# Weights of two small products in two-tile buffers, their splits moved between VectorE and GpSimd, a norm laid out later, and padded operands cleared once

## The chip, the core and the metric

The kernel runs on one core of a Trainium2 chip. A core has TensorE (PE in the profile; PEld is its weight load), VectorE (DVE), ScalarE (ACT), GpSimd (POOL) and SyncE (SP), which here issues the transfers from HBM. SBUF is the working memory of 128 partitions, PSUM holds the products of TensorE in eight banks. The metric is the device time of one execution in microseconds (us), as a median over runs.

## What is computed

One layer of a first model (a gated delta rule beside a linear recurrent unit, then a feed-forward with a squared ReLU) works on 256 tokens of width 1,024. Then 16 learned tokens are put in front, and two layers of a second model follow. The change touches that second model most:

```python
def hybrid_mixer(u, w_in, w_attn_out, conv_w, conv_b, conv_ln_g, conv_ln_b, w_conv_out, w_out):
    proj = u @ w_in
    q, k, v, a, b, g_sb, g_conv = jnp.split(proj, IN_SPLITS, axis=-1)
    y_sb = stick_breaking_attention(q, k, v) @ w_attn_out
    y_conv = conformer_conv(a, b, conv_w, conv_b, conv_ln_g, conv_ln_b) @ w_conv_out
    m = jax.nn.sigmoid(g_sb) * y_sb + jax.nn.sigmoid(g_conv) * y_conv
    return m @ w_out

def second_block(x, meta, ...):
    h = jnp.concatenate([meta_b, x], axis=1)
    for l in range(DEPTH_2):
        h = h + 0.5 * swiglu(rmsnorm_2(h, ffn1_norm[l]), ffn1_w_gate[l], ffn1_w_up[l], ffn1_w_down[l])
        h = h + hybrid_mixer(rmsnorm_2(h, mix_norm[l]), w_in[l], ...)
        h = h + 0.5 * swiglu(rmsnorm_2(h, ffn2_norm[l]), ffn2_w_gate[l], ffn2_w_up[l], ffn2_w_down[l])
    h = rmsnorm_2(h, final_norm)
    return h[:, N_META:]
```

The attention has 8 heads of 64 columns and weighs a key by a sigmoid and the running product of the sigmoids behind it; `conformer_conv` is a gated convolution over 31 tokens, a layer norm and a SiLU. All numbers are float32.

## The kernel before, in words

Everything is held transposed: a tile has 128 features on the partitions and the tokens (256, or 272 with the learned ones) along the free dimension. The residual stream `H` has 8 such tiles and stays in SBUF. A weight tile is 128 by 128.

**Products in three parts.** TensorE multiplies in a reduced float32 format. So each weight tile is split into a high part (`wh`, a copy by ScalarE, line 276) and a low part (`wl`, weight minus high, by VectorE on line 288 or by GpSimd on line 493), and each input too (`x` high and low). One product is three matmuls, high by high, high by low, low by high (lines 534 to 536).

**Jobs and units.** `plan()` lists all products in order as jobs: one job makes one output tile of 128 features. `layout()` cuts a job into units of up to 8 weight tiles (1,024 columns) and packs units into transfers of up to 2,048 columns (`chunks`). Units of `ys` (attention output, `w_attn_out`) and `yc` (convolution output, `w_conv_out`) have only 4 tiles, 512 columns. A job puts its matmuls in a PSUM bank; the first two jobs of `ff1`, of `o2` (output product, `w_out`) and of gate and up are made as a pair, six tiles of each and then two of each.

**Buffers and splits.** There are 5 `wh` and 4 `wl` buffers of 1,024 columns, one per unit in turn. A split is laid out when the unit that is 2 ahead is forced (`MINLEAD`), or up to 3 ahead (`LEAD`) when the plan sees VectorE free. `POOLED` says which units are split on GpSimd: every fourth of the mixer's input products, every second of the list of `ys` and `o2` units, all of `yc`.

**The order of the work** is made while the program is built. Each engine's queue is in order. `op()` keeps a clock per engine with a cost per instruction. The rest of the work, evacuations, norms, attention heads, is written as generators (`flows`); after each weight tile `tick()` lets those go on that are ready by these clocks. `force()` runs flows until a condition holds.

**The stages around the change.** After `o1` (the first layer's output product) `residual` adds into `H`, makes the next input `x` and sums its squares into `acc1`, on GpSimd (`add=pt`). `norm_rows` makes token sums of `acc1` on TensorE (line 319), an inverse root in twelve small VectorE operations, and rows of it by four or six small products. In the mixer the order is `a`/`b`, `q`/`k`, `v`, the gates `gc`, `gs`, then `ys`, `yc`, `o2`. `do_ys` multiplies by a gate out of PSUM; `do_yc` does the same, adds both (SBUF with SBUF) and splits the sum into `mo`, the input of `o2`: a ScalarE copy and a VectorE subtraction. `layer_norm` makes `CO`, the input of `yc`. Behind `o2`, `residual` makes the input of the next gate and up products.

**Padded operands.** Queries of two heads share a tile; `QZ[i]` holds one head of each pair with zeros in the other half. `VZ` holds the values with zero columns between the heads, `AM` the attention weights of the 16 learned tokens with zero rows. All lie in the mixer's arena (`MIX2` columns, opened anew in each layer) and are cleared by GpSimd at its start (lines 1482 to 1484).

Of the kernel before, what the change touches and what calls it, by code (L numbers as in the profile page):

```python
# [23 lines left out]
MIX2 = 16200  # L24
XW = 320
SKEW = ((64, 0), (0, 32))
HSKEW = {"ff1": (56, 32), (0, 0): (56, 16), (1, 0): (56, 32), (0, 1): (56, 48), (1, 1): (56, 16)}
LEAD = 3
# [6 lines left out]
POOLED = [(("a", "b", "q", "k", "v", "gc", "gs"), 4), (("ys", "o2"), 2), (("yc", ), 1), (("o1b",), 2), (("K", "Q"), 8)]  # L35
# [73 lines left out]

def layout():  # L110
# [3 lines left out]
    for j, (_, _, _, _, _, kts) in enumerate(plan()):  # L114
        mine = []
        for ks in kts:
            n = 128 * len(ks)
            limit = 1024 if len(chunks) <= 2 else CHUNK_COLS
            if not chunks or chunks[-1][1] + n > limit:
# [106 lines left out]
def tile_hybrid_blocks(  # L226
# [11 lines left out]
    jobs = plan()  # L238

# [148 lines left out]
    def tick():  # L388
# [8 lines left out]
        while st["split"] < min(st["unit"] + LEAD + 1, len(units)) and clk["V"] < clk["P"] + AHEAD:  # L397
            emit_split(st["split"])
# [64 lines left out]
    for kinds, every in POOLED:  # L463
        mine = [i for i, u in enumerate(units) if jobs[u[0]][0] in kinds]
        on_pool.update(mine[every - 1::every])

    def emit_high(u):
        while st["high"] <= min(u, len(units) - 1):
            i = st["high"]
            _, ks, c, o = units[i]  # L470
            emit_dma(c)
            n = 128 * len(ks)
# [10 lines left out]
    def emit_split(u):  # L483
        while st["split"] <= min(u, len(units) - 1):
            i = st["split"]
            emit_high(i + (i > 0))
            _, ks, c, o = units[i]
            n = 128 * len(ks)
# [12 lines left out]
            if i + 1 < len(units) and units[i + 1][2] != c:  # L501
                raw.pop(c)
                emit_dma(c + RAW - 1)
# [4 lines left out]
    def job(kind, x, n, o=0, bank_=None, last=True, start=None):  # L508
# [14 lines left out]
        for u in mine:  # L523
            st["unit"] = u
            emit_split(u + MINLEAD)
            h, lo = wh.pop(u), wl.pop(u)
            clk["P"] = max(clk["P"], w_at.pop(u) + LAT)
            for i, k in enumerate(units[u][1]):
# [3 lines left out]
                s = slice(128 * i, 128 * i + 128)  # L532
# [795 lines left out]
    start_flow(norm_rows(acc1[:, 0:T1], T1, 1.0 / 1024, 1e-6, R[:, 0:T1], [ev_sq2], ev_r2))  # L1328
# [86 lines left out]

    def swiglu(x, ev_r, o, n, next_g, old_phase, skew, final=False):
# [28 lines left out]
        for m in range(FF2):  # L1445
# [5 lines left out]
            start_flow(evac(ga, ua, m))  # L1451
        x.done()
# [12 lines left out]
    def mixer(x, ev_r, layer, next_g, old_phase):  # L1465
# [9 lines left out]
        QZ = [arena.get(4, n) for _ in range(2)]  # L1475
# [3 lines left out]
        VZ = arena.get(3, 4, 192)  # L1479
        AM = [arena.get(n) for _ in range(2)]  # L1480
        for i in range(2):
            nc.gpsimd.memset(QZ[i].f[64 * (1 - i):64 * (1 - i) + 64], 0.0)  # L1482
# [386 lines left out]
```

## Time and profile before

| | |
|---|---|
| median of 3 runs | 1536.48 us (1528.25 to 1539.7) |
| profiled execution, its own time | 1534.88 us |
| its span, first to last instruction | 1533.2 us |
| mean granted TensorE clock | 0.989 |
| PE busy | 1490.7 us, 97%, 12,120 matmuls |
| VectorE busy | 1075.5 us, 70% |
| ScalarE busy | 802.5 us, 52% |
| GpSimd busy | 196.4 us, 13% |
| HBM read | 245.63 MB |

Busy time of an engine includes the time in which an instruction has begun and is held by something else. A row of the timeline gives start, duration, engine, line, operation, output and inputs, shapes, and in square brackets how long the engine had been idle before it and what it waited for. A row of a window gives a stretch, its length, and for each engine its busy time and the instructions in it, then the granted clock. The matmuls overlap in the pipeline: one of 256 columns is shown with some 0.28 us though they follow each other every 0.11 to 0.12 us, so the pace is read from their count, not from their duration.

### The profile page before, as it was taken

How to read it: one execution, taken by the hardware profiler on the slowest of the kernel's cores; microseconds unless marked ns; L12 is line 12 of the kernel's file. 1: busy time of each engine (PE TensorE's matmuls, PEld its weight loads, DVE VectorE, ACT ScalarE, POOL GpSimd, SP SyncE). 2: the span in 40 equal slices, each digit the busy share in tenths (PEclk: the TensorE clock that was granted, in tenths of full speed). 3: DMA queues.
4: the chain of work that ended last, by engine and by line, in shares of the span. 5: the costliest groups of instructions: out<-in, count | busy, mean ns of one | idle time of the engine just before them, and what ended most of it. 6: DMA issues, size and time to landing. Idle time of an engine off the chain costs nothing. (4 is left out here: it accounts for less than half of the span.)

```text
span 1533.2 us, 29451 instructions
## 1 busy us (share of the span) xinstructions
PE 1490.7 (97%) x12120; PEld 1470.4 (96%) x12120; DVE 1075.5 (70%) x1882; ACT 802.5 (52%) x1365; POOL 196.4 (13%) x236
## 2 busy tenths in 40 slices
PE   7999999999999999999999999999999999899997
PEld 7888999999999999998999999999999989899997
DVE  5986876667666568998866555666558997776654
ACT  4568666544544445555644444444444655555542
POOL 3330300000000012234400000000003235400000
PEclk8999999999999999999999999999999999999998
DMA  5412455554545544433545454554554423455551
GB/s 220 144 56 84 154 204 189 174 190 141 215 166 174 178 171 144 156 114 111 177 182 188 162 177 160 192 184 171 176 186 149 155 110 138 152 207 193 187 181 71
DMA packets 36376, 248.58 MB, mean 162 GB/s; under 512 B 3984, under 2 KB 5264, under 8 KB 12304
## 3 DMA queue, kind: packets, MB, share of 16 engines
q1 hardware_dynamic: 35248, 245.50, 45.3%
q8 instruction: 95, 1.56, 0.4%
q10 hardware_dynamic: 992, 1.19, 0.2%
q14 instruction: 41, 0.34, 0.1%
HBM read 245.63 MB, written 1.05 MB: 161 GB/s over the span
## 5 line engine op out<-in xcount | busy, mean ns | idle before, releaser
L534 PE MATMUL bank<-x,wh 128*128 128x272 f32 (+1 forms) x2752 | 795.8, 289 | 10.7 <-ACT x L276 9.8
L535 PE MATMUL bank<-x,wh 128*128 128x272 f32 (+1 forms) x2752 | 785.3, 285 | 6.5 <-DVE x L288 5.9
L536 PE MATMUL bank<-x,wl 128*128 128x272 f32 (+1 forms) x2752 | 786.8, 286 | 4.2 <-DVE wl L288 3.3
L288 DVE TENSOR_TENSOR wl<-raw,wh 128x1024 fp32r<-128x1024 f32 (+4 forms) x453 | 531.0, 1173 | 191.0 <-PE bank L536 159.5
L276 ACT ACTIVATE wh<-raw 128x1024 fp32r<-128x1024 f32 (+4 forms) x510 | 494.4, 975 | 268.0 <-issue 135.0
L534 PEld LDWEIGHTS bank<-x,wh 128*128 128x128 f32 x2752 | 523.5, 190 | 14.0 <-ACT x L276 10.8
L535 PEld LDWEIGHTS bank<-x,wh 128*128 128x128 f32 x2752 | 524.2, 190 | 9.7 <-DVE x L288 8.0
L536 PEld LDWEIGHTS bank<-x,wl 128*128 128x128 f32 x2752 | 522.0, 190 | 5.5 <-DVE wl L288 4.4
L536 PE MATMUL bank<-hid,wl 128*128 128x272 f32 (+1 forms) x960 | 273.1, 285 | 0.0
L535 PE MATMUL bank<-hid,wh 128*128 128x272 f32 (+1 forms) x960 | 273.0, 284 | 0.0
L534 PE MATMUL bank<-hid,wh 128*128 128x272 f32 (+1 forms) x960 | 272.4, 284 | 0.0
L535 PEld LDWEIGHTS bank<-hid,wh 128*128 128x128 f32 x960 | 181.3, 189 | 0.0
L536 PEld LDWEIGHTS bank<-hid,wl 128*128 128x128 f32 x960 | 180.8, 188 | 0.0
L534 PEld LDWEIGHTS bank<-hid,wh 128*128 128x128 f32 x960 | 180.4, 188 | 0.0
L493 POOL TENSOR_TENSOR wl<-raw,wh 128x512 fp32r<-128x512 f32 (+3 forms) x57 | 106.4, 1878 | 191.9 <-PE bank L536 89.7
L288 DVE TENSOR_TENSOR tmp<-bank,R 128x272 f32<-128x272 f32 (+1 forms) x184 | 78.9, 430 | 66.6 <-PE bank L536 65.8
L276 ACT ACTIVATE tmp<-tmp 128x272 f32<-128x272 f32 (+1 forms) x140 | 59.3, 425 | 114.8 <-DVE tmp L288 78.6
L299 DVE SCALAR_TENSOR_TENSOR bank<-arena,C,bank 128x272 f32<-128x272 f32 (+1 forms) x232 | 102.5, 492 | 3.7 <-ACT bank L276 2.5
L1482 POOL MEMSET arena<- 64x1088 f32 (+1 forms) x4 | 3.9, 976 | 769.0 <-PE bank L536 769.0
L288 DVE TENSOR_TENSOR hid<-tmp,hid 128x272 fp32r<-128x272 f32 (+1 forms) x120 | 51.7, 433 | 38.0 <-ACT hid L276 38.0
L276 ACT ACTIVATE x<-H,C 128x272 fp32r<-128x272 f32 (+2 forms) x64 | 30.0, 487 | 84.7 <-DVE H L288 84.3
L276 ACT ACTIVATE hid<-tmp 128x272 fp32r<-128x272 f32 (+1 forms) x120 | 51.0, 426 | 42.3 <-DVE tmp L288 40.6
(200 smaller groups left out, 950.5 us busy)
## 6 DMA issues: line engine op xcount, KB each, us to landing
raw<-in_w_dram SPq DMA_DIRECT2D x187, 1024.0 KB, 4.8
raw<-in_w_dram SPq DMA_DIRECT2D x32, 960.0 KB, 4.7
raw<-in_w_dram SPq DMA_DIRECT2D x16, 896.0 KB, 4.6
raw<-in_w_dram SPq DMA_DIRECT2D x2, 512.0 KB, 5.9
H<-in_xt_dram SPq DMA_DIRECT2D x1, 544.0 KB, 6.6
LG<-in_lgw_dram SPq DMA_DIRECT2D x1, 512.0 KB, 6.1
out_dram<-H SPq DMA_DIRECT2D x2, 256.0 KB, 2.3
LM<-in_cm_dram SPq DMA_DIRECT2D x1, 320.0 KB, 5.1
```

Source lines behind the costliest of these rows:

```text
L276: nc.scalar.activation(out, in_, func, scale=scale, **kw)
L288: nc.vector.tensor_tensor(out=out, in0=a, in1=b, op=fn)
L299: nc.vector.scalar_tensor_tensor(out=out, in0=a, scalar=s, in1=b, op0=op0, op1=op1)
L493: nc.gpsimd.tensor_tensor(out=lo[:, 0:n], in0=raw[c][:, o:o + n], in1=wh[i][:, 0:n].bitcast(F32), op=SUB)
L534: nc.tensor.matmul(acc, h[:, s], xh, start=first and done == 0, stop=False)
L535: nc.tensor.matmul(acc, h[:, s], xl, start=False, stop=False)
L536: nc.tensor.matmul(acc, lo[:, s], xh, start=False, stop=last and done == total - 1)
L1482: nc.gpsimd.memset(QZ[i].f[64 * (1 - i):64 * (1 - i) + 64], 0.0)
```

## The change

1. `SHARED = ("ys", "yc")`: two jobs in turn of one of these kinds share one pair of buffers of 1,024 columns (a "load"). `layout()` keeps both in one transfer. Splits, look-ahead and `POOLED` now count loads; a product reads its half of the buffer at `o_w`.
2. `POOLED`: `ys` and `o2` are off GpSimd; of `yc`, every second load (of two tiles) stays there, which is two per layer.
3. `residual` behind `o2` sums squares on VectorE (`add=pt` is gone).
4. `norm_rows` behind `o1` is started after the fifth `ff1` job and no longer ahead of `ff1`.
5. `QZ` and `VZ` live in a pool `held` of their own, opened behind `ff2`, and are cleared once, by GpSimd, after the ninth gate/up pair of the first SwiGLU. `AM` is cleared in each mixer as before. `MIX2` falls from 16,200 to 11,800 columns. The pools opened later (`hid` of the SwiGLUs, the mixer's arena) lie higher in SBUF by the size of `held`: 2 x 4 x 272 + 3 x 4 x 192 = 4,480 columns of 4 bytes.

```diff
-MIX2 = 16200
+MIX2 = 11800
+SHARED = ("ys", "yc")
-POOLED = [(("a", "b", "q", "k", "v", "gc", "gs"), 4), (("ys", "o2"), 2), (("yc", ), 1), (("o1b",), 2), (("K", "Q"), 8)]
+POOLED = [(("a", "b", "q", "k", "v", "gc", "gs"), 4), (("yc",), 2), (("o1b",), 2), (("K", "Q"), 8)]
...
+            both = 2 * n if kind in SHARED and nth_of_kind(j) % 2 == 0 else n
+            if not chunks or chunks[-1][1] + both > limit:
...
+    loads, load_of = [], []
+    for u, (j, ks, c, o) in enumerate(units):
+        if jobs[j][0] in SHARED and nth_of_kind(j) % 2:
+            loads[-1][2] += 128 * len(ks)
+            load_of.append((len(loads) - 1, 128 * len(ks)))
+        else:
+            loads.append([c, o, 128 * len(ks), jobs[j][0]])
+            load_of.append((len(loads) - 1, 0))
...
-        while st["split"] < min(st["unit"] + LEAD + 1, len(units)) and clk["V"] < clk["P"] + AHEAD:
+        while st["split"] < min(load_of[st["unit"]][0] + LEAD + 1, len(loads)) and clk["V"] < clk["P"] + AHEAD:
...
-            emit_split(u + MINLEAD)
-            h, lo = wh.pop(u), wl.pop(u)
+            i, o_w = load_of[u]
+            emit_split(i + MINLEAD)
+            h, lo = wh[i], wl[i]
...
-                s = slice(128 * i, 128 * i + 128)
+                s = slice(o_w + 128 * i, o_w + 128 * i + 128)
...
-    start_flow(norm_rows(acc1[:, 0:T1], T1, 1.0 / 1024, 1e-6, R[:, 0:T1], [ev_sq2], ev_r2))
...
+        if m == 4:
+            start_flow(norm_rows(acc1[:, 0:T1], T1, 1.0 / 1024, 1e-6, R[:, 0:T1], [ev_sq2], ev_r2))
...
+    ff1_phase.close()
+    held_pool = ctx.enter_context(tc.tile_pool(name="held", bufs=1))
+    QZ = [held_pool.tile([128, 4, T2], F32, name=f"qz{i}") for i in range(2)]
+    VZ = held_pool.tile([128, 3, 4, 192], F32, name="vz")
+    zeroed = []
+    def zeros():
+        for i in range(2):
+            nc.gpsimd.memset(QZ[i][64 * (1 - i):64 * (1 - i) + 64], 0.0)
+        nc.gpsimd.memset(VZ, 0.0)
...
+            if m == 8 and not zeroed:
+                zeroed.append(True)
+                zeros()
...
-        QZ = [arena.get(4, n) for _ in range(2)]
-        VZ = arena.get(3, 4, 192)
-        for i in range(2):
-            nc.gpsimd.memset(QZ[i].f[64 * (1 - i):64 * (1 - i) + 64], 0.0)
-            nc.gpsimd.memset(AM[i].f, 0.0)
-        nc.gpsimd.memset(VZ.f, 0.0)
+        for a in AM:
+            nc.gpsimd.memset(a.f, 0.0)
...
-            start_flow(residual(b, m, nx, next_g(m), acc1[:, 0:n], ev_sq, o, add=pt))
+            start_flow(residual(b, m, nx, next_g(m), acc1[:, 0:n], ev_sq, o))
```

More of the change, by code (lines that the diff above doesn't have):

```diff
@@ L107, in plan, with nth_of_kind @@
     return jobs
+def nth_of_kind(j):
+    jobs = plan()
+    n = 0
+    while n < j and jobs[j - n - 1][0] == jobs[j][0]:
+        n += 1
+    return n
 def layout():
@@ L113, in layout @@
     off = 0
-    for j, (_, _, _, _, _, kts) in enumerate(plan()):
+    for j, (kind, _, _, _, _, kts) in enumerate(plan()):
         mine = []
@@ L118, in layout @@
             limit = 1024 if len(chunks) <= 2 else CHUNK_COLS
-            if not chunks or chunks[-1][1] + n > limit:
+            both = 2 * n if kind in SHARED and nth_of_kind(j) % 2 == 0 else n
+            if not chunks or chunks[-1][1] + both > limit:
                 if chunks:
@@ L463, in tile_hybrid_blocks @@
     for kinds, every in POOLED:
-        mine = [i for i, u in enumerate(units) if jobs[u[0]][0] in kinds]
+        mine = [i for i, load in enumerate(loads) if load[3] in kinds]
         on_pool.update(mine[every - 1::every])
     def emit_high(u):
-        while st["high"] <= min(u, len(units) - 1):
+        while st["high"] <= min(u, len(loads) - 1):
             i = st["high"]
-            _, ks, c, o = units[i]
+            c, o, n, _ = loads[i]
             emit_dma(c)
-            n = 128 * len(ks)
             h = whp.tile([128, 1024], F32R, tag="wh", name="wh")
@@ L483, in emit_split @@
     def emit_split(u):
-        while st["split"] <= min(u, len(units) - 1):
+        while st["split"] <= min(u, len(loads) - 1):
             i = st["split"]
             emit_high(i + (i > 0))
-            _, ks, c, o = units[i]
-            n = 128 * len(ks)
+            c, o, n, _ = loads[i]
             lo = wlp.tile([128, 1024], F32R, tag="wl", name="wl")
@@ L500, in emit_split @@
             st["split"] += 1
-            if i + 1 < len(units) and units[i + 1][2] != c:
+            if i + 1 < len(loads) and loads[i + 1][0] != c:
                 raw.pop(c)
@@ L1507, in keep_q @@
                 p = slice(64 * i, 64 * i + 64)
-                cp(QZ[i].f[p, t], b[p, 0:n])
+                cp(QZ[i][p, t, 0:n], b[p, 0:n])
             give(b)
@@ L1620, in head @@
                 S = t0 + tn
-                mm(b[:, col:col + S], QZ[par].f[:, hp, t0 - o:t0 - o + 128], KT.f[:, hp, 0:S])
+                mm(b[:, col:col + S], QZ[par][:, hp, t0 - o:t0 - o + 128], KT.f[:, hp, 0:S])
                 col += S
@@ L1672, in head @@
             py = pairs[hp][0]
-            V = VZ.f[:, :, hp, 64 * par:64 * par + 128]
+            V = VZ[:, :, hp, 64 * par:64 * par + 128]
             e = n - 256
```

4 lines of the change are left out of this document (2 added, 2 removed).

## The prediction, made before the change was run

> **What bounds the kernel now.** I read the page first, then the list of what TensorE waited for, then windows around each of those waits, then the order of time on VectorE, GpSimd (POOL) and TensorE inside them.
>
> ```profile
> PE 1490.7 (97%) x12120; PEld 1470.4 (96%) x12120; DVE 1075.5 (70%) x1882; ACT 802.5 (52%) x1365; POOL 196.4 (13%) x236
> ```
>
> TensorE is busy for 97% of the span, and the change takes no product away. It can only win places where TensorE waits or is slowed. These are the windows of the stages that the change touches (columns: length, then busy time and count of PE, PEld, DVE, ACT, POOL, then granted clock, DMA share, GB/s); the first and the last are undisturbed and give the pace.
>
> ```profile
> 390.00:470.00 80.00, 80.00 (x645) 80.00 (x645) 47.63 (x68) 37.95 (x54) 0.00 (x0) 1.00 0.50 183
> 710.70:714.40 3.70, 2.76 (x13) 1.83 (x13) 2.35 (x7) 3.60 (x8) 0.22 (x1) 1.00 0.20 80
> 714.40:733.10 18.70, 17.10 (x122) 16.68 (x122) 17.40 (x27) 9.68 (x19) 10.91 (x8) 0.91 0.46 155
> 1282.70:1305.80 23.10, 22.19 (x194) 21.94 (x194) 17.80 (x32) 15.09 (x28) 15.03 (x11) 1.00 0.46 151
> 1305.80:1323.50 17.70, 11.92 (x74) 11.12 (x74) 14.11 (x20) 8.89 (x16) 8.28 (x5) 0.81 0.48 168
> 1323.50:1337.60 14.10, 14.10 (x122) 14.10 (x121) 9.04 (x14) 7.12 (x15) 6.21 (x6) 1.00 0.36 141
> ```
>
> A product takes 80/645 = 0.124 us at 272 columns and 14.10/122 = 0.116 us at 256. So layer 0 loses 3.7 - 12 x 0.124 = 2.2 us at its first `yc` job and 18.7 - 120 x 0.124 = 3.8 us from there to the second `o2` job; layer 1 loses 23.1 - 192 x 0.116 = 0.9 us over `ys` and `yc`, and 17.7 - 72 x 0.116 = 9.4 us in the first five `o2` jobs (window counts include products cut by the edges). What these losses are made of shows in layer 1, VectorE first, then GpSimd, then TensorE:
>
> ```profile
> 1304.76 0.95 DVE L288 TENSOR_TENSOR wl<-raw,wh 128x768 fp32r<-128x768 f32 x1
> 1305.63 0.42 DVE L288 TENSOR_TENSOR x<-arena,x 128x256 fp32r<-128x256 f32 x1
> 1305.96 0.41 DVE L288 TENSOR_TENSOR arena<-arena,bank 128x256 f32<-128x256 f32 x1
> 1306.41 1.86 DVE L288 TENSOR_TENSOR arena<-arena 128x256 f32<-128x256 f32 x1
> 1308.20 0.41 DVE L288 TENSOR_TENSOR arena<-arena,bank 128x256 f32<-128x256 f32 x1
> 1308.64 0.42 DVE L288 TENSOR_TENSOR arena<-arena 128x256 f32<-128x256 f32 x1
> 1308.98 0.42 DVE L288 TENSOR_TENSOR x<-arena,x 128x256 fp32r<-128x256 f32 x1
> 1306.16 1.83 POOL L493 TENSOR_TENSOR wl<-raw,wh 128x768 fp32r<-128x768 f32 x1 [2.73 <-ACT wh L276]
> 1314.68 2.57 DVE L288 TENSOR_TENSOR x<-arena,x 128x256 fp32r<-128x256 f32 x1
> 1314.58 2.38 POOL L493 TENSOR_TENSOR wl<-raw,wh 128x1024 fp32r<-128x1024 f32 x1 [2.76 <-ACT wh L276]
> 1317.30 0.58 PE L535 MATMUL bank<-x,wh 128*128 128x256 f32 x1 [3.62 <-DVE x L288]
> ```
>
> The same 0.42 us addition takes 1.86 us where a GpSimd split lies over it and ends just after that split; the low half of `mo` takes 2.57 us under a 2.38 us split, and TensorE waits 3.62 us for it. An operation with a PSUM operand is not held:
>
> ```profile
> 718.61 0.42 DVE L288 TENSOR_TENSOR arena<-arena,bank 128x272 f32<-128x272 f32 x1
> 718.35 4.40 POOL L493 TENSOR_TENSOR wl<-raw,wh 128x512 fp32r<-128x512 f32 x3
> ```
>
> So the cost of a GpSimd split in these stages is VectorE's waiting, more than the split. Behind the long waits the clock falls:
>
> ```profile
> 725.20:728.60 3.40, 1.80 (x14) 1.38 (x12) 3.33 (x6) 1.15 (x4) 1.83 (x1) 1.00 0.54 224
> 728.60:732.00 3.40, 3.40 (x15) 3.40 (x16) 3.07 (x8) 2.20 (x6) 0.73 (x1) 0.51 0.37 80
> 1315.70:1319.10 3.40, 1.80 (x8) 1.80 (x9) 2.46 (x2) 1.06 (x1) 1.26 (x1) 0.51 0.27 63
> ```
>
> TensorE busy for 1.80 of 3.4 us was enough to halve the clock in the next 3.4 us, which costs 1.7 us. The Trainium skill ("TensorE: Matmul & The Clock Gate", Part 1) halves the clock after a whole idle window of about 3.4 us; by that rule no halving would be left after this change and the sum below would not move, but the trace halves it earlier, so a leftover wait of near 2 us is priced below with 1.7 us on top.
>
> **The change part by part.**
>
> *First norm moved behind the fifth `ff1` job.* Its token sums stand in TensorE's queue ahead of the third `ff1` job:
>
> ```profile
> 182.78 0.61 PE L319 MATMUL bank<-ones,acc 128*128 128x1 f32 x4 [2.06 <-POOL acc L311]
> ```
>
> Moved past three jobs of 24 products (about 8 us), the sums find `acc1` finished long before; `R2` is read only behind all 32 jobs. VectorE's twelve small operations and the four row products move along and cost the same. Gain 2.1 us, bounds 1.5 to 2.1 (the next weights might be late instead).
>
> *Zeroing once.* At the start of each mixer GpSimd clears two `QZ`, two `AM`, `VZ` and small borders, and only then makes the split of the second `b` tile that is queued behind. GpSimd, then VectorE, then TensorE, layer 0:
>
> ```profile
> 559.58 1.00 POOL L1482 MEMSET arena<- 64x1088 f32 x1 [376.25 <-PE bank L536]
> ...
> 562.13 2.02 POOL L1484 MEMSET arena<- 128x2304 f32 x1
> ...
> 564.47 2.39 POOL L493 TENSOR_TENSOR wl<-raw,wh 128x1024 fp32r<-128x1024 f32 x1
> 561.02 0.50 DVE L299 SCALAR_TENSOR_TENSOR x<-H,C,x 128x272 fp32r<-128x272 f32 x1 [0.59 <-ACT x L276]
> 562.29 0.44 DVE L288 TENSOR_TENSOR acc<-acc,tmp 128x272 f32<-128x272 f32 x1 [0.77 <-ACT tmp L276]
> 564.56 2.33 DVE L293 TENSOR_SCALAR RC<-RC 128x3 f32<-128x3 f32 x1
> 562.02 0.28 PE L535 MATMUL bank<-x,wh 128*128 128x272 f32 x1
> 568.57 0.69 PE L319 MATMUL bank<-M,RC 16*128 16x16 f32 x3 [1.39 <-DVE RC L299]
> ```
>
> The memsets hold nobody (0.50 and 0.44 us beside them), but the split behind them holds the norm's small operation for 2.33 us, and TensorE waits 1.39 us for the norm's rows. Without 1.00 + 1.00 + 2.02 us of memsets the split would start at about 560.5 and end at 562.9. It then lies over the 561.02 operation, the low half of the last input tile, which would end near 563.3; the product that reads it stood at 562.02 and would wait 1.3 us. One wait takes the place of the other: I book 0, in both layers. Bounds: 1.4 us won per layer if the split misses that operation, as much lost if it meets both; 2.8 either way. The memsets go to GpSimd's queue in the first SwiGLU, where the first window above shows POOL at 0.00, and hold nothing.
>
> *`ys` and `yc` in two-tile buffers, `ys` on VectorE, every second `yc` pair on GpSimd.* ScalarE copies half as often (off the path). A split of 1024 columns:
>
> ```profile
> L493 POOL TENSOR_TENSOR wl<-raw,wh 128x1024 fp32r<-128x1024 f32 x25 | 62.9, 2518 | 100.1 <-PE bank L536 68.4 <-ACT wh L276 21.6 <-PE bank L319 8.0
> L288 DVE TENSOR_TENSOR wl<-raw,wh 128x1024 fp32r<-128x1024 f32 x36 | 44.0, 1222 | 22.1 <-PE bank L536 21.3 <-ACT hid L276 0.8
> ```
>
> Per layer VectorE gets four for `ys` and two for `yc`, GpSimd keeps two of 2.5 us. The look-ahead counts buffers, so it reaches twice as far in time here; transfers stay as they are, since four of these tiles fill one of 2,048 columns. Layer 0's `yc` waits for the layer norm, whose chain of small operations is held once now:
>
> ```profile
> 703.93 1.29 POOL L493 TENSOR_TENSOR wl<-raw,wh 128x512 fp32r<-128x512 f32 x1 [2.33 <-DVE rs_y L299]
> 704.04 1.20 DVE L288 TENSOR_TENSOR rs_t<-rs_t,nr 128x3 f32<-128x3 f32 x1
> ```
>
> The first GpSimd `yc` pair gets its buffer when the fourth `ys` job is through, as this split did, and takes 2.5 instead of 1.3 us: I take the 2.2 us of layer 0's first `yc` job to become 3.3, a loss of 1.1 (bounds: 2.2 won, 2.2 lost). In layer 1 nothing waits for that chain, and the 0.9 us go, since no split queues behind a held one (bounds 0 and 0.9).
>
> *`o2` splits and sums of squares on VectorE.* In layer 1 VectorE needs 0.41 + 0.42 + 0.42 = 1.25 us per `yc` job, 10 us for eight, and two splits of 0.95 us, one small one of 0.42 and up to 1.9 us of the 2.5 us that the second GpSimd pair may hold it: 14.2 us from the end of the first job, 1.4 us in. TensorE reaches the last `mo` tile, behind eight jobs of 1.39 us and twelve tiles of the pair (4.2 us), at 15.3. The wait left is near 0.3 us, and about 1.2 us more for the next full split, queued behind that work: 1.5 us for 9.4, a gain of 7.9 with both halved windows gone. Bounds: 3.8 (a rival below) and 9.4. Layer 0 is the same with longer jobs: 1.3 us left of 3.8, a gain of 2.5 (bounds 0.5 and 3.8). Further on VectorE was busy for 9.04 of 14.10 us in the last window; one split and five sums more are 1.2 + 5 x 0.44 = 3.4 us, which fits, and the 2.4 us split over it goes.
>
> *Places in SBUF.* `hid` moves up by 17,920 bytes. Products of one shape run at two paces at full clock:
>
> ```profile
> 1370.00:1430.00 60.00, 60.00 (x532) 60.00 (x531) 39.13 (x57) 31.53 (x45) 0.00 (x0) 1.00 0.54 195
> 1475.00:1515.00 40.00, 40.00 (x338) 40.00 (x337) 23.15 (x32) 18.85 (x26) 0.00 (x0) 1.00 0.35 121
> ```
>
> 0.113 us with `x` and 0.118 with `hid`, and the kernel's pads suggest that addresses decide. With 528 `down` products in each of four SwiGLUs, 0.005 us is 2.6 us apiece, bounds 10 either way. I take 0: all 22 tiles of `hid`, 1,024 or 1,280 bytes apart, keep one pace, so a shift by whole 512 bytes should not matter.
>
> The sum: 2.1 + 0 - 1.1 + 0.9 + 7.9 + 2.5 = 12.3 us, from 1534.9 for the profiled execution (1533.2 its span, 1.7 around it), which is 0.1% under the median of 1536.5: 1523.
>
> **The rivals.** *All waits go* (0.15): the splits miss every chain. 2.1 + 2.8 + 2.2 + 0.9 + 9.4 + 3.8 = 21 us, 1514. For it: VectorE's spare time. Against: two splits stay on GpSimd in the busiest stage.
>
> *The long hold moves on* (0.23): a GpSimd pair holds VectorE for up to 2.4 us while the last `mo` tiles are made, and with 1.7 us for a halved window layer 1 keeps 1.5 + 2.4 + 1.7 = 5.6 of 9.4; layer 0 wins nothing. 2.1 + 0.9 + 3.8 = 6.8 us, 1528. For it: 2518 ns against 1.29 us for a single tile. The Trainium skill ("SBUF — State Buffer", "SBUF: two separate sides") says it as a rule: the port pair is locked for a whole GpSimd instruction that reads SBUF, and a VectorE operation with two SBUF inputs blocks. The rows at 1306.41 and 718.61 agree; it speaks against wider splits on GpSimd.
>
> *VectorE becomes the bound in `o2`* (0.07), the slower side. Per job 1.22 + 0.41 + 0.50 + 0.44 = 2.6 us against 24 x 0.116 = 2.8 of TensorE; it decides once in-order waits for ScalarE (0.59 and 0.77 before the rows of 561.02 and 562.29) fall into it unfilled. All that is added, per layer 0.95 + 0.42 + 3 x 1.22 of splits, 7 x 0.44 of sums and 2.4 for `ys`, would be 10.5 us exposed, 21 in all: 21 - 12.3 = 9 slower, 1544. Against it: 5 us idle in the last window.
>
> *Nothing but the norm and the memsets is felt, or the new places cost what is won* (0.03): 1533.
>
> **How the numbers follow.** My forecast has 0.52 and by itself spans 1516 to 1530. The range from 1512 to 1537 takes in the first two rivals with the spread of the runs (1528 to 1540) and leaves out the slower ones. 1% of the median, what a measurement here can tell from no change, is 15.4 us: below 1521.1 lie the first rival and two fifths of the forecast, 0.36; above 1551.8 only the tail of the third, 0.03; the rest is 0.61.
>
> **What would show it.** The token sums at 182 without idle time; in each mixer's first `a` job a wait of about 1.3 us for the low half of `x`, and no wait before the rows; no VectorE operation stretched behind GpSimd in `o2`, and at most a wait of 1 to 2 us there; a full clock through layer 1's `o2`; layer 0's first `yc` job still short by 2 to 4 us. I am wrong if `o2` jobs wait for `wl` one after another, if 272-column `hid` products leave 0.124 us, or if halved windows stay in both layers.

## The result and the profile after

The changed kernel takes 1523.81 us (median of 10 runs, 1521.81 to 1528.06). The kernel before, timed beside it, takes 1532.55 us (10 runs, 1525.12 to 1539.7). The ratio is 0.995, 95% interval 0.993 to 0.9971: 0.5% faster, which is within the 1% that I had called no change. The time forecast was 1523.0 us. The profiled execution took 1524.07 us with a span of 1522.3 us, against 1533.2: 10.9 us less, where the sum had 12.3.

Lines have moved in the code: the three matmuls of a product stand on lines 552 to 554, VectorE's additions, subtractions and splits on 307, its fused operation on 318, ScalarE's copies on 295, GpSimd's splits on 510, the norm's products on 338. The page of the changed kernel, busy times:

```profile
PE 1488.6 (98%) x12120; PEld 1470.0 (97%) x12120; DVE 1073.5 (71%) x1910; ACT 800.6 (53%) x1349; POOL 136.2 (9%) x189
```

GpSimd lost 60 us of work, and VectorE's busy time fell by 2 us all the same: what it took over in splits is about what it no longer spends held. The windows of the same stages as in the prediction (length, then busy time and count of PE, PEld, DVE, ACT, POOL, clock, DMA share, GB/s): the undisturbed stretch, layer 0's first `yc` job, from there to the second `o2` job, layer 1's `ys` and `yc`, and layer 1's first five `o2` jobs:

```profile
390.00:470.00 80.00, 80.00 (x645) 80.00 (x645) 48.49 (x68) 38.92 (x55) 0.00 (x0) 1.00 0.51 180
709.13:713.12 3.99, 3.99 (x12) 3.24 (x13) 1.74 (x4) 3.48 (x7) 0.00 (x0) 0.50 0.55 230
713.12:729.17 16.05, 16.05 (x121) 16.05 (x121) 13.07 (x29) 6.81 (x13) 0.00 (x0) 0.92 0.10 27
1278.09:1300.70 22.61, 22.61 (x194) 22.61 (x193) 19.70 (x42) 14.50 (x25) 5.23 (x2) 1.00 0.50 183
1300.70:1309.74 9.04, 8.76 (x74) 8.55 (x73) 7.85 (x14) 6.43 (x10) 0.00 (x0) 1.00 0.51 175
```

The last row is the gain: 17.70 us before, 9.04 now, with the clock at 1.00. The second row shows the loss: layer 0's first `yc` job now runs at half clock (1.00 in this window before), behind a wait that is shown below. By stages, from the first product of a stage to the first of the next in each trace; the second column is another execution of the kernel before, taken with the experiments:

| stage | before, us | before, second | after, us | after less first |
|---|---|---|---|---|
| `ff1` | 93.55 | 90.61 | 88.99 | -4.56 |
| `a`, `b` of both layers | 53.71 | 53.73 | 53.25 | -0.46 |
| layer 0, `gs` to `yc` | 64.20 | 65.75 | 68.58 | +4.38 |
| layer 0, `o2` | 27.42 | 25.73 | 23.68 | -3.74 |
| layer 1, `ys` and `yc` | 23.09 | 23.12 | 22.61 | -0.48 |
| layer 1, `o2` | 31.80 | 27.27 | 23.17 | -8.63 |
| last gate and up | 121.24 | 125.54 | 125.16 | +3.92 |
| last `down` and the end | 74.28 | 73.32 | 73.31 | -0.97 |

The 4.38 us of layer 0 from `gs` to `yc` have two parts: `gs` and `ys` together are longer by 2.98 us (52.98 for 50.00), and `yc` by 1.41 us (15.61 for 14.20). Two of these rows, `ff1` and the last gate and up, hold a change of pace that the prediction's sum has at nothing; it is taken up behind the experiments.

**The norm and the zeroing.** The token sums of the moved norm on TensorE, GpSimd's memsets in the first SwiGLU, then at the start of layer 0's mixer the split that moved forward, and what it holds on VectorE and on TensorE:

```profile
189.97 0.50 PE L338 MATMUL bank<-ones,acc 128*128 128x1 f32 x4
...
354.84 2.06 POOL L1444 MEMSET qz<- 64x1088 f32 x2 [164.42 <-PE bank L554]
356.85 2.02 POOL L1445 MEMSET vz<- 128x2304 f32 x1
...
556.09 2.38 POOL L510 TENSOR_TENSOR wl<-raw,wh 128x1024 fp32r<-128x1024 f32 x1
...
556.67 2.10 DVE L318 SCALAR_TENSOR_TENSOR x<-H,C,x 128x272 fp32r<-128x272 f32 x1 [0.59 <-ACT x L295]
...
558.82 0.39 PE L553 MATMUL bank<-x,wh 128*128 128x272 f32 x1 [0.98 <-DVE x L318]
...
564.02 1.03 PE L338 MATMUL bank<-M,RC 16*128 16x16 f32 x6
```

The sums have no bracket: they wait for nothing. The low half of the last input tile now takes 2.10 us under the split instead of 0.50, TensorE waits 0.98 us for it, and the wait of 1.39 us for the norm's rows is gone.

**Layer 0 ahead of `yc`.** VectorE's splits for `ys` and the last operation of the convolution, the layer norm's small operations, GpSimd's two `yc` splits, TensorE and ScalarE:

```profile
684.48 1.22 DVE L307 TENSOR_TENSOR wl<-raw,wh 128x1024 fp32r<-128x1024 f32 x1
...
687.80 1.22 DVE L307 TENSOR_TENSOR wl<-raw,wh 128x1024 fp32r<-128x1024 f32 x1
...
689.82 0.50 DVE L318 SCALAR_TENSOR_TENSOR arena<-arena,C,bank 128x272 f32<-128x272 f32 x1
...
698.00 3.04 POOL L510 TENSOR_TENSOR wl<-raw,wh 128x1024 fp32r<-128x1024 f32 x1 [19.31 <-PE bank L554]
...
700.08 0.99 DVE L314 TENSOR_SCALAR rs_y<-nr 128x3 int32<-128x3 int32 x1
...
702.74 0.16 DVE L318 SCALAR_TENSOR_TENSOR nr<-rs_t,rs_y 128x3 f32<-128x3 f32 x1
...
705.12 1.03 PE L338 MATMUL bank<-M,nr 16*128 16x16 f32 x6
...
705.32 2.35 POOL L510 TENSOR_TENSOR wl<-raw,wh 128x1024 fp32r<-128x1024 f32 x1 [4.28 <-PE bank L554]
...
706.61 2.41 DVE L307 TENSOR_TENSOR arena<-arena,R 128x272 f32<-128x272 f32 x4 [0.95 <-ACT R L295]
...
706.60 1.28 ACT L295 ACT_TABLE_LOAD   x1
708.00 0.61 ACT L295 ACTIVATE arena<-arena,C 128x272 f32<-128x272 f32 x1
708.64 0.43 ACT L295 ACTIVATE x<-arena 128x272 fp32r<-128x272 f32 x1
...
709.13 0.60 PE L552 MATMUL bank<-x,wh 128*128 128x272 f32 x1 [2.98 <-ACT x L295]
```

The layer norm's factors stand ready at 702.90, but the products that lay them out as rows come 2.2 us later on TensorE, which is busy with `ys`. All 96 products of `ys` stand ahead of them and none behind, so TensorE runs dry for 2.98 us. In that time ScalarE copies the rows, loads the table for the SiLU (1.28 us) and makes the first SiLU and the first high part. In the kernel before, the rows' products and the first `yc` product stood here:

```profile
706.30 1.03 PE L319 MATMUL bank<-M,nr 16*128 16x16 f32 x6
...
710.73 0.39 PE L534 MATMUL bank<-x,wh 128*128 128x272 f32 x1
```

Counted from the first `gs` product (660.72 before, 656.15 after) the rows come at 45.6 us before and at 49.0 after. Before, 27 of the 96 `ys` products stood behind them, 27 x 0.124 = 3.3 us of work, and the first `yc` product did not wait.

### The profile page after: what moved, and what is told of

It reads as the page before. It is cut to its first block, busy times and chain, and to the rows that moved or that the text cites. A ratio compares the mean times of both kernels' runs of the same rounds, so it can differ in the third digit from the quotient of the medians.

```text
span 1522.3 us, 29342 instructions
## 1 busy us (share of the span) xinstructions
PE 1488.6 (98%) x12120; PEld 1470.0 (97%) x12120; DVE 1073.5 (71%) x1910; ACT 800.6 (53%) x1349; POOL 136.2 (9%) x189
## 5 line engine op out<-in xcount | busy, mean ns | idle before, releaser
L307 DVE TENSOR_TENSOR wl<-raw,wh 128x1024 fp32r<-128x1024 f32 (+3 forms) x467 | 546.6, 1172 | 194.9 <-PE bank L554 162.8
L552 PEld LDWEIGHTS bank<-x,wh 128*128 128x128 f32 x2752 | 523.1, 190 | 14.0 <-ACT x L295 10.9
L510 POOL TENSOR_TENSOR wl<-raw,wh 128x1024 fp32r<-128x1024 f32 (+1 forms) x27 | 63.8, 2361 | 185.4 <-PE bank L554 116.3
L307 DVE TENSOR_TENSOR tmp<-tmp,bank 128x272 f32<-128x272 f32 (+1 forms) x88 | 38.0, 433 | 38.6 <-ACT tmp L295 38.6
```

The costliest lines, as they stand in the source:

```text
L307: nc.vector.tensor_tensor(out=out, in0=a, in1=b, op=fn)
L510: nc.gpsimd.tensor_tensor(out=lo[:, 0:n], in0=raw[c][:, o:o + n], in1=wh[i][:, 0:n].bitcast(F32), op=SUB)
L552: nc.tensor.matmul(acc, h[:, s], xh, start=first and done == 0, stop=False)
```

## Experiments: one part at a time

**The norm alone.** The kernel before with its first norm moved, nothing else.

```diff
-    start_flow(norm_rows(acc1[:, 0:T1], T1, 1.0 / 1024, 1e-6, R[:, 0:T1], [ev_sq2], ev_r2))
...
+        if m == 4:
+            start_flow(norm_rows(acc1[:, 0:T1], T1, 1.0 / 1024, 1e-6, R[:, 0:T1], [ev_sq2], ev_r2))
```

> The kernel before with only the norm behind o1 started after the fifth ff1 job. If the 2.06 us wait of the token sums was a loss by itself, ff1 gets 2.1 us shorter than before and nothing else moves: about 0.14% faster. The changed kernel's ff1 was 4.6 us shorter (93.55 to 88.99 us). Theory P (pace): the other 2.5 us or so are not the norm but the pace of the 256-column products, 117.8 ns before and 113.3 ns after about 195 us; it can fall either way from one execution to the next, so here ff1 is 2.1 us shorter at 117.8 ns or about 5 us shorter at 113.3 ns. Rival S (order): the moved norm itself sets the faster pace, and ff1 is again near 89 us in this kernel.

Measured: 1527.35 us against 1531.25, ratio 0.9978 (0.9958 to 0.9998). `ff1` takes 91.69 us: 1.86 less than before, not 4.56. So the move is worth about 1.9 us in this pair, and the other 2.7 us of `ff1` in the changed kernel are another thing: theory P, not S.

**Zeroing once, alone.** `QZ` and `VZ` in their own pool, cleared in the first SwiGLU, `MIX2` reduced.

```diff
-MIX2 = 16200
+MIX2 = 11800
+    held_pool = ctx.enter_context(tc.tile_pool(name="held", bufs=1))
...
-        QZ = [arena.get(4, n) for _ in range(2)]
-        VZ = arena.get(3, 4, 192)
```

> The kernel before with only the zeroing changed: QZ and VZ in a pool of their own, cleared once, with the smaller arena. Theory: the split of the second b tile starts four microseconds earlier on GpSimd and holds the low half of the last input tile; TensorE waits about 0.9 to 1.0 us in the first a job of each mixer (as in the changed kernel: 0.98 and 0.87 us) and no longer 1.39 and 1.32 us before the norm's rows. Net 0.5 us faster over both layers, not to be told from no change. Rival: the memsets themselves were the cost, and both waits are gone, 2.7 us faster. hid in its new place: if addresses decide the pace, the down products differ from 124.4 ns (272 columns) by some ns.

Measured: 1532.36 us against 1531.25, ratio 1.0006 (0.9986 to 1.0026). TensorE in layer 0's first `a` job of this kernel:

```profile
559.38 0.39 PE L535 MATMUL bank<-x,wh 128*128 128x272 f32 x1 [0.98 <-DVE x L299]
```

It is the wait of the changed kernel, and the one before the rows is gone. `a` and `b` take 0.21 us less in layer 0 (26.79 to 26.58) and 0.25 less in layer 1 (26.92 to 26.67): one wait in the place of the other. With `hid` at its new addresses the `down` stages keep their 65.71 and 65.73 us, so the addresses cost nothing there.

**The output product alone.** `o2` off GpSimd, its sums of squares on VectorE.

```diff
-POOLED = [..., (("ys", "o2"), 2), ...]
+POOLED = [..., (("ys",), 2), ...]
-            start_flow(residual(b, m, nx, next_g(m), acc1[:, 0:n], ev_sq, o, add=pt))
+            start_flow(residual(b, m, nx, next_g(m), acc1[:, 0:n], ev_sq, o))
```

> The kernel before with only the o2 splits and the sums of squares behind o2 on VectorE; ys and yc as before in single buffers, half of ys and all of yc on GpSimd. Theory L (lock): the o2 stage of layer 1 loses its 9.4 us mostly to the GpSimd splits of o2 itself (1.83 and 2.38 us long), so about 6 of the changed kernel's 8.6 us come back here, and in layer 0 about 2 of 3.7; the yc splits on GpSimd still stretch VectorE. In all about 8 us faster. Rival Y: it is the yc splits on GpSimd that put VectorE behind (eight per layer of 1.3 to 1.5 us), and then only 2 to 3 us come back.

Measured: 1529.22 us against 1531.25, ratio 0.9991 (0.9969 to 1.0013). Layer 1's first five `o2` jobs:

```profile
1303.89:1314.52 10.63, 9.54 (x75) 8.80 (x74) 10.07 (x21) 6.36 (x12) 0.00 (x0) 1.00 0.52 183
```

10.63 us at full clock: the whole stage is 24.76 us, 7.0 less than in the first execution of before and 2.5 less than in the second. Layer 0's stage is 27.66 us, 0.24 more: there it gains nothing. And the last gate and up took 125.16 us, as in the changed kernel, against 121.24. The 8 us expected in all did not come: the medians lie 2.0 us apart, and the interval takes in no change.

**The two-tile buffers alone.** `ys` on VectorE, `yc` as in the change, `o2` and its sums as before.

```diff
+SHARED = ("ys", "yc")
-POOLED = [..., (("ys", "o2"), 2), (("yc", ), 1), ...]
+POOLED = [..., (("o2",), 2), (("yc",), 2), ...]
```

> The kernel before with only the two-tile buffers: ys on VectorE, every second yc pair on GpSimd, o2 as before half on GpSimd. Theory C (chain): in layer 0 the layer norm's result comes later against TensorE, because the wider ys splits stand ahead of it on VectorE; TensorE waits about 3 us at the first yc job as in the changed kernel (2.98 us), with a halved clock behind it, so layer 0 loses 4 us or so, and the ys stage of layer 1 wins 0.9 us. By itself this part is 1 to 4 us slower, or level if o2 in layer 1 gains from an earlier start. Rival: the loss needs the other parts too, and layer 0 stays within 1 us of before.

Measured: 1527.08 us against 1531.25, ratio 0.9975 (0.9953 to 0.9996). Theory C's 1 to 4 us slower, or level, is missed: the medians are 4.2 us lower. In the profiled execution, which took 1531.61 us, layer 1's `ys` and `yc` are 1.3 us shorter than before (21.78 us) and its `o2` takes 28.05 us (31.80 and 27.27 before); where the rest comes from is not shown. Layer 0 is that of the changed kernel: `gs` 33.73, `ys` 19.24 with the wait of 2.98 us, `yc` 16.06, and `o2` 23.68. So this part alone, the buffers with the splits of `ys` and `yc` moved, makes layer 0's loss, and alone makes the gain in its `o2`, although every second `o2` split is still on GpSimd. In layer 1 the held subtraction is still there (VectorE, then GpSimd):

```profile
1312.85 2.57 DVE L307 TENSOR_TENSOR x<-arena,x 128x256 fp32r<-128x256 f32 x1
...
1312.75 2.38 POOL L510 TENSOR_TENSOR wl<-raw,wh 128x1024 fp32r<-128x1024 f32 x1 [2.76 <-ACT wh L295]
```

## Experiments: what layer 0 lost

The prediction had put this loss on a GpSimd split of two tiles that holds VectorE. The rival is the order in the queues: VectorE's wider splits ahead of the convolution's end, and the rows' products further back on TensorE.

**All `yc` splits on VectorE.**

```diff
-POOLED = [..., (("yc",), 2), (("o1b",), 2), ...]
+POOLED = [..., (("o1b",), 2), ...]
```

> The changed kernel with all four yc pairs of each layer split on VectorE, none on GpSimd. In layer 0 of the changed kernel TensorE waits 2.98 us at 709.1 for the high half of the convolution's output, and the clock is halved beside it; ys and yc take 19.24 + 15.61 = 34.85 us. Theory H: the wait is made of GpSimd's yc pairs, which hold the layer norm's small operation (0.99 us) and the multiplication behind it (1.35 us where 0.44 us is usual): without them about 1.8 us of the wait go, the halved stretch shrinks too, and ys + yc come to 31 to 33 us. Theory V: the wait comes from VectorE's own queue, where splits of 1.22 us stand ahead of the convolution's last operations, and from the place of the norm's products in TensorE's queue: two more splits of 1.22 us leave the wait at 2.9 us or more, and ys + yc at 34.5 us or more. Layer 1 (ys + yc 22.6, o2 23.2 us) should not move by more than 0.5 us by either.

Measured: 1525.32 us against 1534.45, ratio 0.9936 (0.9911 to 0.996). `ys` and `yc` take 34.43 us. VectorE's last small operation of the layer norm, and TensorE:

```profile
699.35 0.16 DVE L318 SCALAR_TENSOR_TENSOR nr<-rs_t,rs_y 128x3 f32<-128x3 f32 x1
...
702.53 1.03 PE L338 MATMUL bank<-M,nr 16*128 16x16 f32 x6
706.44 0.59 PE L552 MATMUL bank<-x,wh 128*128 128x272 f32 x1 [2.87 <-ACT x L295]
```

Nothing is held any more, the factors are ready 0.8 us earlier after the first `gs` product (45.9 us, 46.75 in the changed kernel), and the rows' products stand at 49.0 us all the same, behind all of `ys`. The wait is 2.87 us for 2.98. The hold on VectorE is not what makes it; the place in TensorE's queue is. That the held multiplications (2.41 us in the changed kernel, 1.50 here) cost only 0.1 us agrees with the rows of the changed kernel: they lie beside ScalarE's table load. Theory H falls for this stage. Layer 1 moved by a little more than the 0.5 us allowed: `ys` and `yc` are 0.8 us shorter, `o2` 0.55 longer.

**`ys` in single tiles again, `yc` in two.**

```diff
-SHARED = ("ys", "yc")
+SHARED = ("yc",)
-POOLED = [..., (("yc",), 2), (("o1b",), 2), ...]
+POOLED = [..., (("ys",), 2), (("yc",), 2), (("o1b",), 2), ...]
```

> The changed kernel with ys in single tiles again, every second of them split on GpSimd as before, and yc alone in buffers of two. Theory V: the three splits of 1.22 us for ys ahead of the end of layer 0's convolution make the longer wait; without them gs + ys + yc of layer 0 come back from 68.6 us to about the 64.2 us of the kernel before, while o2, whose first splits are no longer queued behind single yc splits, keeps its 23.7 us (27.4 before): some 4 us less than the changed kernel's span for this layer. Theory H: the yc pairs on GpSimd make the wait: gs + ys + yc stay at 67 us or more. A third, that it is the reach of the look-ahead over both, would take the gain in o2 away again (27 us) together with the loss.

Measured: 1530.17 us against 1534.45, ratio 0.9968 (0.9944 to 0.9992): slower than the changed kernel (1524.74 in the same set of runs). `gs` to `yc` takes 71.89 us. Theory V's 64.2 is missed; H's 67 or more is met, but not by H's cause. TensorE's waits in layer 0, then VectorE:

```profile
704.36 0.39 PE L552 MATMUL bank<-x,wh 128*128 128x272 f32 x1 [0.46 <-ACT x L295]
711.97 0.60 PE L553 MATMUL bank<-x,wh 128*128 128x272 f32 x1 [7.21 <-DVE x L307]
...
708.19 1.23 DVE L307 TENSOR_TENSOR wl<-raw,wh 128x1024 fp32r<-128x1024 f32 x1 [4.66 <-ACT wh L295]
...
709.68 3.29 DVE L307 TENSOR_TENSOR x<-arena,x 128x272 fp32r<-128x272 f32 x4
```

The rows' products are back in their old place (45.6 us), and the wait for the first high half is 0.46 us: that much was right. But the look-ahead, which counts buffers, had put the third `yc` split ahead of the four low halves in VectorE's queue. Its high part is a ScalarE copy that stands behind the SiLU of all four tiles. So VectorE idles for 4.66 us while one finished input after another, four in the end, stands behind the waiting split, and TensorE idles for 7.21 us. `o2` keeps 23.68 us. The third theory had named the reach of the look-ahead, but with another effect: it expected 27 us in `o2`.

**The look-ahead in tiles again, `ys` single.** The kernel above, with the look-ahead mended; the second `b` split is moved too (see below).

```diff
-        while st["split"] < min(load_of[st["unit"]][0] + LEAD + 1, len(loads)) and ...:
+        while st["split"] < load_of[min(st["unit"] + LEAD, len(units) - 1)][0] + 1 and ...:
...
-            emit_split(i + MINLEAD)
+            emit_split(load_of[min(u + MINLEAD, len(units) - 1)][0])
```

> The kernel with ys in single tiles and yc in buffers of two, where TensorE lost 7.21 us in layer 0's second yc job, with two edits: the look-ahead of the splits counts tiles again and not buffers, and the second b tile is split on VectorE. The trace of that kernel showed VectorE idle for 4.66 us at 703.5, waiting for ScalarE's copy for a yc pair that the look-ahead had queued ahead of the low halves of the convolution's output. Theory Q (the order in the queues): the products that lay out the norm's rows stay where they were in the kernel before (24 products ahead of their place in the changed kernel), the low halves now stand ahead of that split, and the 7.21 us go to under 1.5 us: gs + ys + yc of layer 0 come to 64 to 66 us (68.6 in the changed kernel), o2 to 23.7 to 25 us, and a + b are 1.1 us shorter; in all 4 to 6 us less than the changed kernel. Theory H (GpSimd's wide splits hold VectorE): one of the two yc pairs on GpSimd still lies over these operations, and gs + ys + yc stay at 67 us or more.

Measured: 1522.41 us against 1534.42, ratio 0.9916 (0.9886 to 0.9946). Layer 0's first `yc` job as a window, and TensorE's waits in it:

```profile
708.89:712.63 3.74, 2.90 (x13) 1.90 (x13) 2.28 (x5) 3.65 (x8) 0.71 (x1) 1.00 0.58 171
...
708.89 0.39 PE L554 MATMUL bank<-x,wh 128*128 128x272 f32 x1 [0.46 <-ACT x L295]
709.95 0.39 PE L555 MATMUL bank<-x,wh 128*128 128x272 f32 x1 [0.66 <-DVE x L307]
```

The 7.21 us are 0.66, `gs` to `yc` takes 64.28 us (68.58 in the changed kernel, 64.20 before), `o2` 24.64. A GpSimd `yc` split of two tiles still lies beside it (706.58 to 709.60). Theory Q of the order in the queues holds. From `ff2` on the profiled execution is 4.7 us shorter than that of the changed kernel, of which 2.2 us lie in the `a` and `b` jobs. What is left of the first job, 3.74 us for 1.49, is ScalarE's: SiLU and high half of a tile come every 0.97 us, four times.

**The look-ahead in tiles, both in two-tile buffers.** The changed kernel with the same edit of the look-ahead and of the `b` split, `SHARED` and `POOLED` as the change has them.

```diff
-            emit_split(i + MINLEAD)
+            emit_split(load_of[min(u + MINLEAD, len(units) - 1)][0])
```

> The changed kernel, ys and yc both in buffers of two, with the look-ahead counting tiles again and the second b tile split on VectorE. Fewer splits of 1.22 us stand ahead of the convolution's last operations and the low halves stand ahead of the next yc split; the rows' products come 6 products later than in the kernel before instead of 27. Theory Q: the wait of 2.98 us in layer 0's first yc job shrinks in that proportion, to about 1 us, and gs + ys + yc come to 65 to 66.5 us with o2 at 23.7 us. If it is the width of the ys splits alone, whatever their order, gs + ys + yc stay at 67.5 us or more.

Measured: 1521.58 us against 1534.42, ratio 0.9918 (0.9887 to 0.9949), the lowest time of all. `gs` to `yc` is 66.23 us, `o2` 24.55 (23.7 expected). 21 `ys` products stand behind the rows' products again, and the wait for the first high half is 0.26 us, but another has come in `ys`; TensorE, and then the windows of the first `yc` job and of what follows up to the third `o2` job:

```profile
703.08 0.39 PE L556 MATMUL bank<-x,wl 128*128 128x272 f32 x1 [1.89 <-DVE wl L307]
...
707.30:711.05 3.75, 3.25 (x12) 2.00 (x13) 1.90 (x5) 3.65 (x8) 0.00 (x0) 1.00 0.71 267
711.05:727.15 16.10, 15.97 (x129) 15.76 (x127) 14.68 (x29) 7.42 (x16) 2.49 (x1) 1.00 0.18 67
```

With the shorter look-ahead a `ys` split of two tiles is 1.89 us late. The clock stays whole: in both kernels the trace has no halved clock between 79 and 1511 us. That the `b` split, moved in both, makes the difference is ruled out by the next experiment, which has it alone: there no `ys` product stands behind the rows' products, the wait is 2.98 us, and `gs` to `yc` takes 68.96 us. Beside the unaltered changed kernel (ratio 0.9938, 0.9913 to 0.9963, below) their intervals overlap, so that they beat it is likely from the stages and not settled by the times.

**The second `b` split of each mixer on VectorE.** The changed kernel with the split behind the memsets moved off GpSimd.

```diff
+    firsts = [i for i, load in enumerate(loads) if load[3] == "b"]
+    on_pool.difference_update(firsts[1::4])
```

> The changed kernel with the second b tile of each mixer split on VectorE instead of GpSimd. By my account of the zeroing, the wait before the first a job of each mixer (0.98 us at 558.8, 0.87 us at 1148.6) is that split holding the low half of the last input tile. Then both waits go and the norm's rows do not wait either: a and b together take 1.0 us less in layer 0 and 0.9 us less in layer 1 (26.6 to 25.6 and 26.7 to 25.8 us), with no other stage moved. The rival is that the split of 1.2 us on VectorE itself stands ahead of that operation: then the wait stays near 1 us or the rows get it, and a and b keep 26.5 us or more.

Measured: 1523.21 us against 1534.45, ratio 0.992 (0.9898 to 0.9942). VectorE in layer 0's first `a` job:

```profile
556.89 1.22 DVE L307 TENSOR_TENSOR wl<-raw,wh 128x1024 fp32r<-128x1024 f32 x1
558.02 0.50 DVE L318 SCALAR_TENSOR_TENSOR x<-H,C,x 128x272 fp32r<-128x272 f32 x1
```

The low half takes 0.50 us again and TensorE waits neither for it nor for the rows; `a` and `b` take 25.44 us (26.58) and 25.63 (26.67). So the split made the wait in its new place. That it made the old wait too rests on the prediction's row at 564.56, where it lies over the norm's operation.

## Experiments: the same program twice

**The changed kernel again.**

> The changed kernel once more, unaltered, for what differs between two executions of one program. If the pace of 256-column products in ff1 (113.3 or 117.8 ns each) and in the last gate and up jobs (121.2 or 125.2 us for that stage) is set by the program, both stages show the lengths of the first profile, 89.0 and 125.2 us, to 0.1 us. If it settles afresh in each execution, one of them differs by 1 to 6 us while the waits elsewhere (2.98 us in layer 0's first yc job, 0.28 us in layer 1's o2) stay as they were.

Measured: 1524.74 us against 1534.45, ratio 0.9938 (0.9913 to 0.9963). Every stage from `ff1` on agrees with the first profile to 0.05 us, but for layer 0's `yc` (15.19 for 15.61 us): `ff1` 88.98, last gate and up 125.16, the waits 2.98 and 0.29 us. In `yc` it is the place of the half clock that differs: here it begins by 705.3 us, 1.2 us before the wait ends at 706.49, and in the first profile 0.3 us before, so that less of it falls on products. The span is 1519.3 us, 3.0 less than the first profile's; 2.0 us of it lie in the first layer's input products, which the change doesn't touch.

**The kernel before again.**

> The kernel before once more, unaltered, for what of its first profile is of one execution only. If the program sets the pace of the 256-column products and the waits in o2, ff1 takes 93.6 us again, layer 1's o2 31.8 us with its 3.6 us wait, and layer 1's gate and up jobs 121.2 us. If ff1 comes out between 90.6 and 95.2 us, as in the kernels that share its instructions up to there, or layer 1's o2 at 27 to 28 us, these are of the execution, and the change's gain there varies with them.

Measured: 1531.46 us against 1534.42 of the other runs of the same program, ratio 0.9984 (0.9957 to 1.0012). Its profiled execution has a span of 1526.8 us, 6.4 less than the first one of the same program. Layer 1's first five `o2` jobs, then the low half of `mo` on VectorE and the split on GpSimd that had held it:

```profile
1300.64:1313.77 13.13, 11.00 (x74) 10.26 (x73) 10.90 (x18) 6.58 (x12) 6.87 (x4) 0.87 0.40 141
...
1309.42 0.42 DVE L288 TENSOR_TENSOR x<-arena,x 128x256 fp32r<-128x256 f32 x1
...
1309.46 6.00 POOL L493 TENSOR_TENSOR wl<-raw,wh 128x1024 fp32r<-128x1024 f32 x2 [2.89 <-PE bank L536]
```

Here VectorE begins 0.04 us ahead of GpSimd and takes 0.42 us. In the execution that the prediction read, GpSimd began at 1314.58 and VectorE at 1314.68, and the same operation took 2.57 us. The stage is 27.27 us instead of 31.80. So 4.5 us of the kernel before hang on which of two instructions comes first by a tenth of a microsecond. The norm alone had the short form (VectorE 0.29 us ahead, 0.42 us, stage 27.29), the zeroing alone the long one (GpSimd 0.11 us ahead, 2.57 us, stage 31.84), and the two-tile buffers alone the long operation too, as shown above.

The pace of the 256-column products differs too. The same two stretches, in `ff1` and in the last gate and up, of the kernel before in its first execution (the second of its rows stands in the prediction), in its second, and of the changed kernel:

```profile
200.00:260.00 60.00, 60.00 (x512) 60.00 (x511) 39.83 (x63) 37.87 (x64) 0.00 (x0) 1.00 0.52 184
```

```profile
200.00:260.00 60.00, 60.00 (x532) 60.00 (x531) 41.91 (x67) 39.68 (x67) 0.00 (x0) 1.00 0.55 194
1370.00:1430.00 60.00, 60.00 (x511) 60.00 (x511) 37.88 (x55) 30.34 (x43) 0.00 (x0) 1.00 0.55 189
```

```profile
200.00:260.00 60.00, 60.00 (x532) 60.00 (x531) 41.94 (x67) 39.57 (x67) 0.00 (x0) 1.00 0.53 194
1370.00:1430.00 60.00, 60.00 (x512) 60.00 (x511) 37.75 (x55) 30.77 (x44) 0.00 (x0) 1.00 0.51 180
```

532 or 512 products in 60 us, 0.113 or 0.117 us each, at a full clock and without a wait, in the same jobs of the same program. This is the 2.7 us of `ff1` that the move of the norm didn't give: unmoved, the stage took 93.55 or 90.6 us, moved, 91.7 or 88.99. Compared within a pace, the move is worth 1.6 to 1.9 us. Once it took 95.17, with the two-tile buffers alone, and that is not a third pace: there the clock was 0.50 from 183.05 to 186.40 us, behind the same wait of some 2.06 us for the token sums that left it whole in the other four executions with the norm unmoved.

What sets the pace stays open. In all thirteen profiled executions `ff1` begins at the slower pace, and where the faster one comes, it comes behind the norm's small products. The addresses in SBUF don't decide it alone: they are the same in both executions of the kernel before. But the last gate and up had the slower pace in all eight executions with `o2` off GpSimd, and in one of five with half of `o2` there. So these 3.9 us may in part be a price of the change, which no run here separates.

## Why the prediction was right or wrong

**The time** came out 0.8 us from the forecast, and that is luck in part. The sum started from an execution of 1534.9 us, 2.4 above the median of 1532.55, and its gain of 12.3 us is too large: the medians lie 8.7 us apart. The two errors cancel. Between the first profiles the span fell by 10.9 us, with layer 0 2.0 us short of its terms and the rest nearly even; between the second ones, 1526.8 and 1519.3 us, it fell by 7.5.

**The norm, 2.1 us:** right in kind, 1.6 to 1.9 us measured, within its bounds. The weights behind it came no later. What I had not priced is the half clock that its wait brought in one execution of five, 1.6 us more.

**The zeroing, 0:** right, by the step as I gave it. The split moved forward, held the low half of the last input tile for 2.10 us, and 0.98 us (I had 1.3) took the place of 1.39. Each layer won 0.2 us. The memsets in the first SwiGLU cost nothing that shows.

**Layer 0's first `yc` job, a loss of 1.1 us with bounds of 2.2:** wrong, and the step that failed is the chain I costed. From `gs` to `yc` 4.4 us were lost, a wait of 2.98 us ahead of the job and 1.4 us of half clock in `yc`. Against the second execution of before it is 2.8 us, since there one stretch of half clock (708.95 to 712.30) lies in `yc`, where the first execution had it in `o2`. With `o2` the layer lost 0.6 and 0.8 us, where I had 1.4 us won. I had asked how long GpSimd's wider split would hold the norm's small operations. It did hold two of them, by 0.8 and 0.9 us, but with all holds gone the wait was 2.87 us instead of 2.98. I had not followed what wider splits and a look-ahead in buffers do to the order of the queues: VectorE got two splits of 1.22 us between the convolution's last operations, the last of which begins 1.8 us later after the first `gs` product (33.67 and 31.85 us), and the rows' products were laid out 27 `ys` products further back, with none left behind them to cover ScalarE's work. "The look-ahead counts buffers, so it reaches twice as far in time here" stands in the prediction and has no price there. It is the term that was missing: with the look-ahead in tiles the loss against the first execution of before is 0.1 us (`ys` single) or 2.0 (both), for 4.4; against the second it is a gain of 1.5 or a loss of 0.5, for 2.8. So the reach is the larger part where `ys` has two tiles, and the wait of 1.89 us for one of its wider splits is about as long as the rest.

**Layer 0's `o2`, a gain of 2.5 us:** 3.7 measured against the first execution and 2.1 against the second, within the bounds, but not for the reason given. I had it from the `o2` splits on VectorE; these alone gave -0.24 us, and the buffers alone 3.74. The single `yc` splits on GpSimd are the likely cause: three low halves of `mo` are stretched to 0.95, 1.53 and 1.53 us in the kernel with `o2` alone off GpSimd, and to at most 0.76 with the buffers alone. No run changes these splits and nothing else, and 0.9 us of the gain go when the look-ahead counts tiles (24.55 and 24.64 us for 23.68).

**Layer 1's `o2`, a gain of 7.9 us:** 8.6 measured against the execution I had read, with 0.3 us of wait left for 1.5, and both halved windows gone. The reason was right: `o2`'s splits and sums on VectorE alone gave 7.0. But against the second execution of before the same step is worth 4.1 us, and `o2` alone 2.5. The row of 2.57 us, the largest single cause in my sum, was one outcome of a race, which three of the five executions with `o2` splits on GpSimd show.

**Layer 1's `ys` and `yc`, 0.9 us:** no wait is left (22.61 of 22.61 us busy), and 0.5 came out, because `yc` ran at the slower pace (11.31 us for 10.88).

**Places, 0:** right for `hid`; the `down` stages of 272 columns kept their time. The guess that addresses decide between the two paces of 256-column products does not hold, since one program with the same addresses had both; the 3.9 us which the last gate and up took longer come from the pace, and their cause is open.

**The rivals.** The long hold did not move on: no subtraction into `mo` is stretched in the changed kernel. VectorE did not become the bound: 7.85 of 9.04 us in the first five `o2` jobs, without a growing wait. "All waits go" is refuted by the 2.98 us. On the Trainium skill ("SBUF — State Buffer", "SBUF: two separate sides"): the lock of the port pair agrees with the rows at 556.67 and 706.61, operations with two inputs from SBUF beside a GpSimd split (556.09 to 558.47 and 705.32 to 707.67). The row at 700.08 has one input and took 0.99 us for 0.17 under a split, so two inputs were not needed here; why is not shown. The Trainium skill says too that whichever of the two starts first gets the pair for its whole instruction; the race agrees, where VectorE came 0.04 us first, kept its 0.42 us, and the two GpSimd splits behind it show 6.00 us where 2 x 2.38 is usual. On the clock rule of the Trainium skill ("TensorE: Matmul & The Clock Gate", Part 1): a wait of 2.98 us, shorter than its idle window of about 3.4, was followed by the half clock of the second row of the windows, so less idle time was enough here than the rule asks for. The half clock cost 1.2 us from the second `yc` job on (16.05 us to the second `o2` job for 120 x 0.124 = 14.9), and little in the first (3.99 us, against 3.74 and 3.75 at full clock), which waited for ScalarE anyway.

## What to carry to other kernels

When a buffer is made to hold two units, everything that counts buffers changes its meaning: look ahead, due times and the shares given to an engine. Price the order that comes out, the instruction at the head of each in-order queue and what stands finished behind it, before the cost of the wider instruction itself. And read a second execution before booking a wait of several microseconds: where two instructions start 0.1 us apart and contend, the trace shows one outcome of a race, and here the other one was worth half as much.

## What was not expected of the hardware

Products of 256 columns run at 0.113 or 0.117 us at full clock and without waits; a stretch keeps its pace over 60 us and more, and the same jobs of one program had the other pace in another execution (532 and 512 in the windows above). It is worth 2.7 to 3.9 us in each of two stages. Products of 272 columns kept 0.124 us in all runs.

The length of a wait does not tell by itself whether the clock is halved. A wait of 2.98 us was followed by the half clock and one of 1.89 us was not (the windows of the kernel with both in two tiles have the clock at 1.00). The wait of some 2.06 us ahead of `ff1`'s token sums was, in one execution of five. Nor does the busy share of a stretch tell: in the kernel before, TensorE was busy for 1.62 us from 179.1 to 182.5 and the clock stayed at 1.00, while in its second execution it was busy for 2.54 us from 705.5 to 708.9 and the clock was 0.50 for the next 3.4 us. Where the limit lies is open.
